# The last two modulation sets of layer two as VectorE sums over feature chunks, in a planned kernel on one core

## Chip, core and metric

One NeuronCore of a Trainium2 chip runs the whole program in one launch. The metric is the device time of one execution in microseconds. Times of instructions, waits and transfers come from one execution that the hardware profiler recorded.

## What is computed

The program is a block of two transformer layers over 256 latent tokens (`x`) and 256 context tokens (`ctx`), followed by a second network of mixers and cross-attention. The part that matters here is the first block, cut down:

```python
silu_c, silu_cc = jax.nn.silu(c), jax.nn.silu(c_ctx)[None]       # 1 x 1024 each
for l in range(2):
    need_ctx = l < 1
    mod   = silu_c  @ w_ada[l] + b_ada[l]                         # 1024 x 6144 weights
    mod_c = silu_cc @ w_ada[l] + b_ada[l]
    sh1, sc1, g1, sh2, sc2, g2 = jnp.split(mod, 6, axis=-1)
    h = modulate(rms_norm(x, norm1_g[l]), sh1, sc1)               # likewise hc from mod_c
    y, yc = mixer_sublayer(h, hc, ..., need_ctx)                  # w_in, attention, branches, w_out
    x = x + g1 * y
    h = modulate(rms_norm(x, norm2_g[l]), sh2, sc2)
    x = x + g2 * expert_choice_ffn(h, ...)                        # 16 experts of 1024 x 1024, three matrices each
    if need_ctx:                                                  # layer one only
        ...                                                       # the same for the context tokens
```

`w_ada[l]` is 24 MB and is used for two vectors alone. Its 6144 columns are six modulation vectors of 1024. The kernel takes them in three sets of two: set 0 is `sh1, sc1`, set 1 is `g1, sh2`, set 2 is `sc2, g2`. In layer two the context tokens need set 0 only, since nothing after their keys and values is computed.

## The kernel before

**The planner.** The kernel writes no order of its own. Every operation goes to a planner (class `Plan`), which builds the graph of dependencies, gives each operation a modelled cost on each engine that may run it, and places all of them by list scheduling on five queues: TensorE, ScalarE, VectorE, GpSimd, and SyncE, which issues the transfers. `copy` may go to ScalarE or VectorE, `binary` to VectorE or GpSimd, `scaled` to ScalarE or VectorE; the planner chooses. The real instructions are all issued from one line of `issue`, line 461, so that the profile shows L461 everywhere and groups are told apart by tile names.

**Weights.** Each weight tile is 1 MB (8 KB per partition) and comes through the ring `W`, which has six buffers (`BUFS`, line 40). `split_stream` loads a tile, calls `step()`, which takes one unit of background work, and splits each 128x512 slice into a rounded half `wh` (a copy, on ScalarE or VectorE) and the rest `wl` (a subtraction, on VectorE or GpSimd). `linear` then makes three products with 512 columns for each slice and each half of the tokens. In the experts the weights go to TensorE unsplit, and the ring is longer: `wring` names the tiles that are free then, 14 in layer one (line 1607) and 17 in layer two (line 1638), six of them `W`.

**Modulation.** `ada_units` gives eight units for a set. Four of them load two tiles of 128x2048 (two `W` buffers) and make 8 products on TensorE: a weight of 128x32, `scT`, which holds both vectors (latent and context), against 512 columns of `w_ada`; the four column groups go to four row groups of one PSUM bank, `acc`. In the trace each such product is two MATMUL records. After the eighth unit, `ada_finish` copies the bank to SBUF on ScalarE, makes four transposes (128x128), four more in `ada_pairs` (the order of features that the router and experts use), and adds biases on VectorE for both streams.

**The stage.** The two sets of layer two that the change touches are background work of layer two's dense stage, 940 to 1217 us of the trace: `dense` makes the queries, keys and values (`w_in`), the attention (about 1020 to 1064 us), the gates and branches, and the product with `w_out`, which needs set 1. Before it stand layer one's dense stages (to 440 us) and its experts (440 to 938 us), after it layer two's experts (1217 to 1650 us) and the second network. The units are hung in at line 1630:

```python
self.bg, self.bgrate = self.ada_units(1, (1, 2)), 1
self.dense(1, 0, xs, hi, lo, self.z_tiles(1536), ctx_prep, lambda: self.mem_norm(0))
```

## Time and profile before

| | |
|---|---|
| runs | 2045.97, 2048.46, 2048.66 us; median 2048.46 |
| the profiled execution | 2050.08 us, its span 2048.3 us |
| TensorE busy (PE) | 1815.9 us, 89% |
| VectorE busy (DVE) | 881.5 us, 43% |
| ScalarE busy (ACT) | 855.3 us, 42% |
| GpSimd busy (POOL) | 300.9 us, 15% |
| moved by DMA | 611.72 MB, mean 299 GB/s |
| granted TensorE clock, mean | 0.937 of full speed |

The stages differ: in the dense stages TensorE is busy nearly all the time, in the experts the transfers run without a break. A share over the whole span hides that; the profile's table by stage, further down, is the one to read. The profiled execution lies 1.62 us above the median of the runs.

### The profile page before, as it was taken

What the parts mean: (1) busy time and instruction counts of PE and PEld (TensorE: products, weight loads), DVE (VectorE), ACT (ScalarE), POOL (GpSimd) and SP (SyncE); (2) the same over time, 40 slices, a digit from 0 to 9 for tenths busy, and PEclk for the clock granted to TensorE, in tenths of its full rate; (3) what the DMA queues carried; (4) which work ended last, traced back from release to release, by engine and by line L of the source; (5) the groups of instructions that cost most, each with busy time, mean ns of one, the idle gap of its engine ahead of it and who ended that gap; (6) DMA issues with size and microseconds to landing.
All of it is one profiled execution on the core that took longest, in us unless ns stands there. A gap on an engine that the chain in (4) does not pass through costs nothing.

```text
span 2048.3 us, 29471 instructions
## 1 busy us (share of the span) xinstructions
PE 1815.9 (89%) x11570; PEld 1148.4 (56%) x11570; DVE 881.5 (43%) x1855; ACT 855.3 (42%) x1895; POOL 300.9 (15%) x387
## 2 busy tenths in 40 slices
PE   7999999999999898878899997666766689999997
PEld 4677767774443232224677774322322268889886
DVE  3766686680020100206765650101000057867775
ACT  3664676562232121114575541101110046776765
POOL 1202250230000000003500300000000023312421
PEclk9999999999999999999999998866667789999999
DMA  9767663678989999998647889999999975436330
GB/s 367 264 224 273 228 237 129 224 274 317 409 368 374 422 402 422 421 421 323 230 183 289 288 338 421 421 421 420 421 421 421 421 275 150 140 119 192 123 124 32
DMA packets 150347, 611.72 MB, mean 299 GB/s; under 512 B 10144, under 2 KB 32320, under 8 KB 96192
## 3 DMA queue, kind: packets, MB, share of 16 engines
q1 hardware_dynamic: 150208, 609.84, 77.5%
q8 instruction: 91, 1.49, 0.3%
q14 instruction: 48, 0.39, 0.1%
HBM read 606.63 MB, written 3.16 MB: 298 GB/s over the span
## 4 chain that ended last, share of the span: by engine, by line
PE 57%; DMA 30%; DVE 7%; POOL 2%; ACT 2%; issue 1%; SPq 0%; POOLq 0%; DVEq 0%; ACTq 0%
PE lin L461 43%; PE aux L461 13%; DMA W<-w_gate_e 5%; DMA W<-w_up_e 4%; DMA W<-w_down_e 3%; PE acc L461 2%; DMA HL<-w_gate_e 2%; DMA OL<-w_up_e 2%; DMA G<-w_down_e 2%; DVE wl L461 2%; DMA M<-w_gate_e 2%; DMA G<-w_gate_e 2%; DMA KC<-w_down_e 1%; POOL sm L461 1%; DVE S L461 1%
## 5 line engine op out<-in xcount | busy, mean ns | idle before, releaser
L461 DVE TENSOR_TENSOR wl<-W,wh 128x512 fp32r<-128x512 f32 (+1 forms) x514 | 360.3, 705 | 162.9 <-ACT wh L461 159.3
L461 ACT ACTIVATE wh<-W 128x512 fp32r<-128x512 f32 (+1 forms) x482 | 291.3, 607 | 241.4 <-PE lin L461 186.5
L461 DVE TENSOR_TENSOR S<-lin,S 128x512 f32<-128x512 f32 (+1 forms) x32 | 17.9, 558 | 596.6 <-PE lin L461 581.5
L461 ACT ACTIVATE S<-lin 32x512 f32<-32x512 f32 (+2 forms) x94 | 52.3, 556 | 421.8 <-PE lin L461 421.0
L461 POOL TENSOR_TENSOR wl<-W,wh 128x512 fp32r<-128x512 f32 (+1 forms) x62 | 80.6, 1302 | 947.7 <-DMA W<-w_in 412.9
L461 PE MATMUL lin<-wl,HH 128*128 128x512 f32 (+1 forms) x600 | 205.6, 394 | 2.8 <-DVE wl L461 2.8
L461 PE MATMUL lin<-wh,HL 128*128 128x512 f32 (+1 forms) x600 | 204.0, 393 | 0.7 <-DVE HL L461 0.7
L461 PE MATMUL lin<-wh,HH 128*128 128x512 f32 (+1 forms) x600 | 203.8, 392 | 0.8 <-ACT wh L461 0.5
L461 PE MATMUL lin<-W,S 128*32 128x256 f32 (+1 forms) x1288 | 149.5, 512 | 49.5 <-DMA W<-w_up_e 14.2
L461 PE MATMUL aux<-cst,S 128*128 128x128 f32 x604 | 116.1, 287 | 23.0 <-DVE S L461 18.4
L461 PEld LDWEIGHTS lin<-W,S 128*32 128x32 f32 (+1 forms) x1288 | 50.7, 133 | 134.3 <-issue 47.3
L461 ACT ACTIVATE S<-aux 128x512 f32<-128x512 f32 (+5 forms) x139 | 66.6, 485 | 141.0 <-PE aux L461 139.7
L461 PEld LDWEIGHTS lin<-wl,HH 128*128 128x128 f32 x600 | 107.9, 189 | 27.9 <-DVE wl L461 8.1
L461 PEld LDWEIGHTS aux<-cst,S 128*128 128x128 f32 x604 | 79.5, 154 | 73.6 <-DVE S L461 42.1
L461 PEld LDWEIGHTS lin<-wh,HH 128*128 128x128 f32 x600 | 108.5, 189 | 20.9 <-issue 3.4
L461 PEld LDWEIGHTS lin<-wh,HL 128*128 128x128 f32 x600 | 108.9, 189 | 18.1 <-DVE HL L461 1.3
L461 PE MATMUL lin<-wh,OL 128*128 128x512 f32 x272 | 93.9, 396 | 0.0
L461 POOL TENSOR_SCALAR sm<-sm 128x1 f32<-128x1 f32 (+3 forms) x42 | 17.1, 407 | 466.3 <-ACT G L461 392.5
L461 ACT ACTIVATE S<-aux,sm 128x256 f32<-128x256 f32 (+2 forms) x136 | 71.4, 529 | 15.4 <-DVE sm L461 12.9
L461 PE MATMUL lin<-wl,OH 128*128 128x512 f32 x208 | 75.5, 402 | 2.4 <-DVE wl L461 2.2
L461 PE MATMUL lin<-wh,OH 128*128 128x512 f32 x208 | 76.2, 403 | 0.0
L461 PE MATMUL lin<-W,HL 128*64 128x512 f32 x288 | 68.4, 601 | 7.4 <-DMA W<-w_up_e 4.7
(430 smaller groups left out, 3264.0 us busy)
## 6 DMA issues: line engine op xcount, KB each, us to landing
W<-w_in SPq DMA_DIRECT2D x62, 1024.0 KB, 7.2
W<-w_up_e SPq DMA_DIRECT2D x50, 1024.0 KB, 18.6
W<-w_gate_e SPq DMA_DIRECT2D x50, 1024.0 KB, 18.7
W<-w_down_e SPq DMA_DIRECT2D x49, 1024.0 KB, 19.7
W<-w_ada SPq DMA_DIRECT2D x40, 1024.0 KB, 5.0
W<-w_in SPq DMA_DIRECT2D x32, 768.0 KB, 4.7
W<-w_out SPq DMA_DIRECT2D x20, 1024.0 KB, 5.1
Z<-w_down_e SPq DMA_DIRECT2D x17, 1024.0 KB, 19.8
```

Of the source, the lines that this page charges most:

```text
L461: fn(*(self.real(a) for a in args), **{k: self.real(a) for k, a in kw.items()})
```

## The change

Sets 1 and 2 of layer two are computed for the latent stream alone, in another way. `ada_sums` gives eight units for a set (two column halves of 1024, four units each). A unit loads one tile with two feature chunks of 128 x 1024 columns (1 MB, one `W` buffer) and VectorE multiplies each by the latent vector's value on its partition and adds it into a tile `ac` (128x1024, two buffers). After four units `ada_block` sums over the partitions on TensorE: for each 128 columns one product with `ac` as the weight and a 128x2 column of ones. Eight products give the half; eight more give the pair order for the half that needs it, so that a set has 24 products and both sets 48. `ada_done` adds the biases straight from PSUM. The copy on ScalarE, the transposes and the context stream's half are gone; `modT[1]` is set to zero once at the start, since the gates' transpose still reads both streams. `ac` takes the 8 KB of one `W` buffer: the ring `W` goes from six to five, everywhere, and the experts' rings from 14 to 13 and from 17 to 16 tiles.

```diff
-BUFS = {"W": (2048, 6), "HH": (2048, 1), "HL": (2048, 1), "OH": (2048, 1), "OL": (2048, 1), "Z0": (2048, 1), "Z1": (2048, 1),
+BUFS = {"W": (2048, 5), "HH": (2048, 1), "HL": (2048, 1), "OH": (2048, 1), "OL": (2048, 1), "Z0": (2048, 1), "Z1": (2048, 1),
...
-        "M": (2304, 1),
+        "M": (2304, 1), "ac": (1024, 2),
...
+        nc.vector.memset(self.modT[1], 0.0)
...
+    def ada_sums(self, r):
...
+        def unit(g, h):
+            if g == 0 and h == 0:
+                box["ps"] = self.acc_ps()
+            if h == 0:
+                box["a"] = self.t([128, 1024], F32, "ac")
+            acc = box["a"]
+            w = self.wload(src, 2 * h, 2, r * 2048 + 1024 * g, 1024)
+            for k in range(2):
+                sc = self.scT[:, 2 * h + k, 0:1]
+                if h or k:
+                    nc.vector.scalar_tensor_tensor(out=acc, in0=w[:, k], scalar=sc, in1=acc, op0=ALU.mult, op1=ALU.add)
+                else:
+                    nc.vector.tensor_scalar(out=acc, in0=w[:, k], scalar1=sc, scalar2=None, op0=ALU.mult)
+            if h == 3:
+                self.ada_block(r, g, acc, box["ps"])
+                if g:
+                    self.ada_done(r, box["ps"])
+        return [lambda g=g, h=h: unit(g, h) for g in range(2) for h in range(4)]
+
+    def ada_block(self, r, g, acc, ps):
...
+        for i in range(8):
+            o = 16 * g + 2 * i
+            self.nc.tensor.matmul(ps[:, o:o + 2], acc[:, 128 * i:128 * i + 128], self.ones2, start=True, stop=True, skip_group_check=True)
+        if g == (r == 1):
+            e = acc.rearrange("p (a q j) -> p a j q", a=4, j=2)
+            for i in range(8):
+                o = 32 + 2 * i
+                self.nc.tensor.matmul(ps[:, o:o + 2], e[:, i // 2, i % 2], self.ones2, start=True, stop=True, skip_group_check=True)
+
+    def ada_done(self, r, ps):
...
+        nc.vector.tensor_tensor(out=self.modT[1][:, cs, 0], in0=v[:, 0:16], in1=self.sml("b_ada", 48, 48)[:, cs], op=ALU.add)
+        o = (self.B2 if r == 1 else self.A2)[1][:, 0, :]
+        nc.vector.tensor_tensor(out=o, in0=v[:, 16:24], in1=self.sml("b2p", 16 + 8 * (r - 1), 8), op=ALU.add)
+        if r == 2:
+            nc.vector.scalar_tensor_tensor(out=o, in0=o, scalar=1.0, in1=self.sml("norm2p", 8, 8), op0=ALU.add, op1=ALU.mult)
+        self.ada_scales(1, r, (0,))
...
-        self.wring = ["DFT", "M", "W", "W", "W", "W", "W", "W", "Z1", "OH", "OL", "Z0", "G0", "G1"]
+        self.wring = ["DFT", "M", "W", "W", "W", "W", "W", "Z1", "OH", "OL", "Z0", "G0", "G1"]
...
-        self.bg, self.bgrate = self.ada_units(1, (1, 2)), 1
+        self.bg, self.bgrate = self.ada_sums(1) + self.ada_sums(2), 1
...
-        self.wring = ["DFT", "M", "KC", "W", "W", "W", "W", "W", "W", "Z1", "OH", "OL", "HL", "HH", "Z0", "G0", "G1"]
+        self.wring = ["DFT", "M", "KC", "W", "W", "W", "W", "W", "Z1", "OH", "OL", "HL", "HH", "Z0", "G0", "G1"]
```

The planner lays the whole program out anew. On TensorE, just ahead of the attention of layer two (the last products of the keys and queries, then the transposes `aux<-cst`; `lin`, `aux` and `acc` are PSUM banks, the number behind a name is its buffer and use), the queue before has six groups of the set's products:

```order
L461 MATMUL lin_1_220<-wh_0_200,HL_5_5599 128x512
L461 MATMUL acc_0_129<-W_3_342,scT 32x512 x4
L461 MATMUL acc_0_129<-W_4_371,scT 32x512 x4
L461 MATMUL aux_3_122<-cst,M_0_485 128x128
L461 MATMUL aux_1_340<-cst,S_2_853 128x128 x2
L461 MATMUL acc_0_129<-W_1_181,scT 32x512 x4
L461 MATMUL acc_0_129<-W_2_323,scT 32x512 x4
L461 MATMUL acc_0_129<-W_5_417,scT 32x512 x4
L461 MATMUL acc_0_129<-W_0_165,scT 32x512 x4
L461 MATMUL aux_2_119<-cst,M_0_485 128x128 x2
L461 MATMUL aux_3_122<-cst,S_0_483 128x128 x4
```

And now, at the same place:

```order
L461 MATMUL lin_1_221<-wh_0_201,HL_5_5600 128x512
L461 MATMUL acc_0_130<-ones_69,ac_0_5524 128x2
L461 MATMUL lin_2_278<-wh_1_203,HH_5_5590 128x512
L461 MATMUL lin_0_218<-wh_1_203,HH_5_5590 128x512
L461 MATMUL acc_0_130<-ones_69,ac_0_5524 128x2 x5
L461 MATMUL aux_1_341<-cst,S_2_870 128x128 x2
L461 MATMUL aux_3_123<-cst,M_0_507 128x128
L461 MATMUL acc_0_130<-ones_69,ac_0_5524 128x2
L461 MATMUL lin_2_278<-wl_1_228,HH_5_5590 128x512
L461 MATMUL aux_2_120<-cst,M_0_507 128x128
```

The groups of four products with 512 columns are gone from here, and products with two columns stand among the linear products, each of them reading an `ac` tile.

On VectorE, in the attention of layer two (the reductions and reciprocals are the softmax's, `OL<-aux` is attention output, `wl` a weight's rest, `S<-S,sm` the softmax's scaling), the queue before reads:

```order
L461 TENSOR_REDUCE sm_9_529<-aux_1_340 128x1
L461 TENSOR_TENSOR wl_1_227<-W_3_342,wh_1_202 128x512
L461 TENSOR_REDUCE sm_12_540<-aux_2_119 128x1
L461 RECIPROCAL sm_11_519<-sm_10_543 128x1
L461 TENSOR_TENSOR OL_19_6059<-aux_3_122,OH_20_6052 128x256
L461 TENSOR_SCALAR S_2_208<-S_2_208,sm_11_519 128x512
L461 TENSOR_REDUCE sm_18_818<-aux_1_340 128x1
L461 TENSOR_REDUCE sm_15_807<-aux_3_122 128x1
L461 TENSOR_TENSOR OL_19_6059<-aux_0_177,OH_20_6052 128x256
L461 RECIPROCAL sm_14_798<-sm_13_780 128x1
L461 TENSOR_TENSOR wl_2_215<-W_4_371,wh_2_205 128x512
```

And now, some rows into the same softmax:

```order
L461 SCALAR_TENSOR_TENSOR ac_1_5852<-W_3_343,scT,ac_1_5852 128x1024
L461 TENSOR_REDUCE sm_15_804<-aux_3_123 128x1
L461 TENSOR_REDUCE sm_18_826<-aux_1_341 128x1
L461 RECIPROCAL sm_14_798<-sm_13_788 128x1
L461 SCALAR_TENSOR_TENSOR ac_1_5852<-W_0_166,scT,ac_1_5852 128x1024
L461 RECIPROCAL sm_17_820<-sm_16_815 128x1
L461 RECIPROCAL sm_20_848<-sm_19_837 128x1
L461 TENSOR_REDUCE sm_21_857<-aux_3_123 128x1
L461 TENSOR_REDUCE sm_0_100<-aux_1_341 128x1
L461 SCALAR_TENSOR_TENSOR ac_1_5852<-W_0_166,scT,ac_1_5852 128x1024
L461 COPY S_2_870<-aux_0_178 128x4x128
L461 SCALAR_TENSOR_TENSOR ac_1_5852<-W_2_324,scT,ac_1_5852 128x1024
```

Sums into `ac` stand between the reductions, where subtractions for weights and scalings stood; most of these went to GpSimd and ScalarE.

On the transfers' queue, where layer two's dense stage ends and the experts' weights begin (`W_n` are the ring's buffers, the other names tiles that are free by then), before:

```order
L461 DMA W_3_342<-w_down_e 128x2048
L461 DMA W_4_371<-w_down_e 128x2048
L461 DMA kv<-QB_5_7492 128x1024
L461 DMA W_5_417<-w_down_e 128x2048
L461 DMA QB_6_7569<-w_gate_e 128x1024
L461 DMA W_0_165<-w_down_e 128x2048
L461 DMA M_0_485<-w_down_e 128x2048
L461 DMA G_24_7630<-w_up_e 128x2048
L461 DMA G_20_7659<-w_up_e 128x2048
L461 DMA DFT_17_7686<-w_down_e 128x2048
L461 DMA KC_5_7712<-w_down_e 128x2048
L461 DMA W_1_181<-w_down_e 128x2048
```

And now:

```order
L461 DMA W_4_372<-w_up_e 128x2048
L461 DMA W_0_166<-w_down_e 128x2048
L461 DMA kv<-QB_5_7491 128x1024
L461 DMA W_1_182<-w_down_e 128x2048
L461 DMA QB_6_7557<-w_gate_e 128x1024
L461 DMA W_2_324<-w_down_e 128x2048
L461 DMA M_0_507<-w_down_e 128x2048
L461 DMA G_25_7627<-w_up_e 128x2048
L461 DMA G_21_7656<-w_up_e 128x2048
L461 DMA DFT_18_7683<-w_up_e 128x2048
L461 DMA KC_5_7709<-w_down_e 128x2048
L461 DMA W_0_166<-w_gate_e 128x2048
```

Before, the names go round the six buffers, W_5 among them; now the ring comes back to W_0 after W_4, and by the end of the excerpt a buffer (W_0) is given out for the second time, which the excerpt of before does not do.

## Rows read from the trace of the kernel before

**Rows 1.** Busy time by stage; the first line names the columns.

```profile
core 0: us, PE busy (x) PEld busy (x) DVE busy (x) ACT busy (x) POOL busy (x), PEclk, DMA share, GB/s
635.00:938.00 303.00, 260.96 (x1136) 86.16 (x1134) 29.32 (x46) 48.37 (x88) 0.00 (x0) 0.98 1.00 415
946.00:1020.00 74.00, 66.16 (x331) 47.09 (x330) 59.56 (x109) 46.95 (x95) 44.44 (x71) 0.98 0.71 258
1020.00:1064.00 44.00, 44.00 (x309) 35.99 (x309) 34.35 (x85) 36.12 (x86) 3.36 (x3) 1.00 0.40 144
1064.00:1217.00 153.00, 151.46 (x892) 116.94 (x895) 93.48 (x184) 83.98 (x162) 25.17 (x25) 1.00 0.81 297
1217.00:1650.00 433.00, 303.03 (x3170) 129.59 (x3164) 26.40 (x47) 49.53 (x128) 2.56 (x4) 0.74 1.01 420
1650.00:2048.30 398.30, 377.45 (x2456) 330.92 (x2448) 291.69 (x633) 268.81 (x653) 107.63 (x141) 0.98 0.43 137
```

**Rows 2.** Instructions writing acc in 900 to 1250 us: min/median/max ns, first and last start.

```profile
L461 PE MATMUL acc<-W,scT x128: 592/592/617, 973.2 to 1142.4; 128*32 128x512 f32 x128
```

**Rows 3.** TensorE in order of time: start, duration, idle before and its releaser.

```profile
1005.80 3.64 PE L461 MATMUL acc<-W,scT 128*32 128x512 f32 x32
1012.18 0.44 PE L461 MATMUL aux<-cst,M 128*128 128x128 f32 x2 [2.74 <-DVE KC L461]
1014.96 1.25 PE L461 MATMUL aux<-DFT,S 128*128 128x128 f32 x4 [1.78 <-DVE QB L461]
```

**Rows 4.** The same view in the experts of layer one, and in the attention of layer two.

```profile
526.57 1.05 PE L461 MATMUL aux<-ones,S 128*128 128x2 f32 x8
527.55 1.08 PE L461 MATMUL lin<-G,HH 128*64 128x512 f32 x4
...
554.67 0.38 PE L461 MATMUL aux<-ones,S 128*128 128x2 f32 x2
554.98 1.94 PE L461 MATMUL lin<-W,S 128*64 128x512 f32 x8
...
1025.69 0.60 PE L461 MATMUL aux<-cst,S 128*128 128x128 f32 x4
1026.05 0.48 PE L461 MATMUL aux<-KC,QA 128*128 128x256 f32 x2
```

**Rows 5.** VectorE and GpSimd groups by shape, whole span: busy us, mean ns, idle before.

```profile
L461 DVE SCALAR_TENSOR_TENSOR S<-x,sm,KC 128x1024 f32<-128x1024 f32 x2 | 2.6, 1284 | 1.3 <-POOL sm L461 1.3
...
L461 DVE TENSOR_SCALAR Z<-XC,sm 128x1024 f32<-128x1024 f32 x2 | 1.5, 754 | 5.4 <-POOL sm L461 5.4
...
L461 DVE TENSOR_SCALAR Z<-x,sm 128x1024 f32<-128x1024 f32 x3 | 4.2, 1406 | 1.2 <-POOL sm L461 1.2
...
L461 DVE TENSOR_TENSOR wl<-W,wh 128x512 fp32r<-128x512 f32 x396 | 292.8, 743 | 135.2 <-ACT wh L461 131.8 <-DMA W<-w_br_global 0.5 <-issue 0.2
...
L461 DVE CAST wh<-W 128x512 fp32r<-128x512 f32 x76 | 37.8, 499 | 7.6 <-PE lin L461 6.6 <-PE aux L461 0.2
...
L461 DVE TENSOR_SCALAR S<-S,sm 128x512 f32<-128x512 f32 x27 | 13.3, 496 | 0.7
...
L461 POOL TENSOR_TENSOR wl<-W,wh 128x512 fp32r<-128x512 f32 x52 | 70.0, 1350 | 522.7 <-ACT wh L461 347.2 <-DVE wh L461 175.4
```

**Rows 6.** Busy time in two stretches of ten us in the experts of layer one.

```profile
580.00:590.00 10.00, 10.00 (x47) 3.32 (x45) 5.84 (x9) 4.95 (x9) 0.00 (x0) 1.00 0.61 253
...
620.00:630.00 10.00, 10.00 (x48) 3.38 (x46) 0.00 (x0) 2.96 (x7) 0.00 (x0) 1.00 0.53 197
```

**Rows 7.** The DMA queue's own waits, 540 to 640 us: total us, times, longest.

```profile
SPq L461 <- PE lin L461: 68.5, 8, 13.6
```

**Rows 8.** Busy time at the start of the experts of layer two.

```profile
1200.00:1210.00 10.00, 10.00 (x63) 7.62 (x63) 3.39 (x7) 3.64 (x7) 0.00 (x0) 1.00 0.72 265
...
1220.00:1230.00 10.00, 10.00 (x186) 5.93 (x178) 0.85 (x2) 1.94 (x6) 0.00 (x0) 1.00 0.99 412
```

**Rows 9.** The DMA queue's own waits, 1150 to 1217 us.

```profile
SPq L461 <- DVE wl L461: 17.2, 5, 7.1
```

**Rows 10.** VectorE's waits for a weight load, 940 to 1215 us.

```profile
DVE wl L461 <- DMA W<-w_br_global: 0.5, 1, 0.5
```

More of the change, by code (lines that the diff above doesn't have):

```diff
@@ L873, in ada_units @@
         return units
+    def ada_sums(self, r):
+        nc = self.nc
+        src = self.A["w_ada"][1]
+        box = {}
+        def unit(g, h):
[26 more added lines that the diff above has]
+    def ada_done(self, r, ps):
+        nc = self.nc
+        cs = slice(r * 16, r * 16 + 16)
+        v = ps[:, 0:48].rearrange("p (i w) -> p i w", w=2)[:, :, 0]
+        nc.vector.tensor_tensor(out=self.modT[1][:, cs, 0], in0=v[:, 0:16], in1=self.sml("b_ada", 48, 48)[:, cs], op=ALU.add)
[4 more added lines that the diff above has]
+        self.ada_scales(1, r, (0,))
     def ada_first(self):
@@ L927, in ada_finish, with ada_scales @@
             nc.vector.tensor_tensor(out=o, in0=i0, in1=b, op=ALU.add)
-        for s in range(2):
+        self.ada_scales(l, r, (0, 1))
+    def ada_scales(self, l, r, streams):
+        nc = self.nc
+        mod = self.modT[l]
+        for s in streams:
             if r == 0:
```

## The prediction

> **What bounds the kernel now.** I read the table by stage first, since the shares of the whole span mix stages with different limits [rows 1]. Two stages run at the transfers' rate: the end of layer one's experts (635 to 938 us, DMA share 1.00 at 415 GB/s) and layer two's experts (1217 to 1650 us, 1.01 at 420 GB/s); TensorE is busy 261 of 303 and 303 of 433 us there, so what ends them is the bytes still to come. Layer two's dense stage, where the change sits, goes by TensorE once attention has begun: 44.00 of 44 us from 1020, 151.46 of 153 from 1064. Ahead of the attention, 946 to 1020, it is mixed: TensorE 66.16 of 74, VectorE 59.56, and the last waits there, 2.74 us for VectorE's KC and 1.78 us for its QB, stand right behind two groups of modulation products [rows 3]. In that stretch VectorE's chain, not TensorE's work, sets when attention starts. Then I looked at where the six W buffers matter: as lead for weights in the dense stages, and as part of the ring that holds expert weights when an expert stage begins.
>
> **TensorE.** The old sets are 128 records [rows 2], 8 groups of 16; two groups last 3.64 us [rows 3], so a group is 1.82 us and all are 14.6 us. Their 16 transposes go by the row of other 128x128 products, four records starting 0.36 us before the next work, 0.09 us each [rows 4]: 1.4 us. Added are 48 products of two columns. The row of such products (`ones`) has eight records, two for each product, that take 0.98 us up to the next start [rows 4], 0.245 us a product; two records alone take 0.31 us. 48 x 0.245 = 11.8 us, at most 14.9. Net -14.6 - 1.4 + 11.8 = **-4.2 us** (-1.1 at the dear price). Where it lies matters: the first old group starts at 973.2 us and the first four stand ahead of attention, where by the new order only 8 of the 48 products stand. Ahead of attention that is -7.3 + 2.0 = -5.3 us on an engine that already waits for VectorE; behind it -7.3 - 1.4 + 9.8 = +1.1 us on an engine that is full.
>
> **VectorE.** 32 operations of 128x1024 are new: 28 multiply-and-add, 4 multiply. The trace has two multiply-and-adds of that shape at 1284 ns; a multiply of that shape takes 754 ns in one group and 1406 ns in another [rows 5]. I take 1284 and 754, since the operands (SBUF, a scalar for each partition) are those of these rows: 36.0 + 3.0 = 39.0 us, 41.6 with 1406. In exchange the planner moves 18 subtractions `wl` to GpSimd (743 ns each on VectorE, 1350 ns there [rows 5]) and takes over 9 casts `wh` from ScalarE at 499 ns. Dense stage in sum: 39.0 - 13.4 + 4.5 = **+30 us** on VectorE, and 18 x 1.35 = +24 us on GpSimd. By the order it falls so. Ahead of attention: 9 x 1.284 + 2 x 0.754 - 3 x 0.743 + 2 x 0.499 = +11.9 us, on 59.56 of 74: 71.5 of 74. In attention: 12 x 1.284 + 0.754 - 9 x 0.743 - 11 scalings x 0.496 (to ScalarE) + 6 x 0.499 = +7.0 us, on 34.35 of 44: 41.4 of 44. Later: +5.7 on 93.48 of 153, which has room. Each time it just fits. But VectorE's queue is in order: a sum that waits for its 1 MB tile, or runs, holds the softmax's reductions and reciprocals behind it, and TensorE waits for those. So the 5.3 us that TensorE gets back ahead of attention I cost at nothing: they end at VectorE, whose 14.4 us of idle time become 2.5. Bounds: -5 if the cover holds, +9 if one sum of 1.284 us in three of the 21 up to the end of attention delays TensorE by its own length.
>
> Here GpSimd and VectorE would work side by side more than before. In 946 to 1020 us they were busy 59.56 + 44.44 = 104 us in 74, so at least 30 us overlapped [rows 1]; the trace shows no general exclusion between them. The Trainium skill's page "SBUF — State Buffer" states under "Who interferes with whom" that the port pair these two engines share is an exclusive lock, and that a VectorE instruction with two SBUF inputs contends with a GpSimd instruction that reads SBUF. The added multiply-and-adds are such instructions, and so are the subtractions moved to GpSimd, so the rule speaks against the change; the 30 us say that it can't hold for everything both run. What it would cost is rival D.
>
> **The transfers.** The bytes of the two sets are the same, 16 tiles of 1 MB. Layer two's dense stage uses two W buffers for a pair of tiles before and one a unit after, with five in the ring. Its weights are early now: between 940 and 1215 us VectorE waited for a weight tile once, 0.5 us [rows 10]. With five buffers I take +1 us for this and all other dense stages and the second network (-2 to +4; five sixths of a lead that hardly ever runs out).
>
> The experts are another matter. Before their unbroken stretch the transfers stop because the ring is full: 253 GB/s in 580 to 590 us and 197 in 620 to 630 [rows 6], the transfers' queue waiting 68.5 us in eight waits for TensorE's `lin` products to release tiles [rows 7]. From 635 us on nothing stops them until the stage's end. A tile less in the ring is 1.049 MB less held when that stretch begins, and at 0.42 MB/us (420 GB/s) that is **2.5 us** later at the end. In layer two the queue waits 17.2 us for VectorE's `wl` (W tiles still in use by the dense stage) before 1217 us [rows 9], the rate is 265 GB/s in 1200 to 1210 and 412 from 1220 on [rows 8]: again a tile less, **2.5 us**. Bounds 0 (another tile comes free in time, or a full ring wasn't what held the last tile back) to 5 each.
>
> **The sum.** Dense stage of layer two: 0 ahead of and in attention, +1.1 behind it; experts +2.5 and +2.5; other stages +1: +7.1 us on the profiled execution's 2050.08 = 2057.2. That execution lies 1.62 us above the median, so the forecast for the median is **2055.5 us**, 0.3% slower.
>
> **Rivals.** (B) The VectorE work does fit into its idle time, so TensorE's -4.2 counts, and the experts' +5 balance it: about 2049.3, no change. For it: VectorE stays at 71.5 of 74 and 41.4 of 44 and the order was laid out for just that. Against it: the planner's modelled costs, and waits right ahead of attention that are VectorE's now. (C) The other side: TensorE's gain is larger than its net, because some 12 of the 48 small products fall into idle time it has anyway (7.8 us ahead of attention), -4.2 - 12 x 0.245 = -7.1, and the experts lose nothing since the tile that is missing wasn't the last to come free: about 2041.4, faster. It decides if the experts' unbroken stretches begin as early, measured from the stage's start, as before. (D) GpSimd and VectorE stop each other: while a sum runs, a GpSimd subtraction doesn't. Up to the end of attention 21 sums of 1.284 us are 27 us; GpSimd was busy 44.44 + 3.36 = 47.8 of those 118 us, 0.40, so 0.40 x 27 = 10.9 us of waiting more, and TensorE waits for these `wl`. On the forecast: about 2066.4. It decides if the mean of GpSimd's `wl` rises well over 1350 ns or the sums over 1284. By the skill's rule named above this is the expected case; the 30 us of overlap are against its full size.
>
> **How the numbers follow.** A 0.42, B 0.24, C 0.20, D 0.14. The range reaches from C's inner edge to D: C lies at 2041.4 with an upper half that reaches 2044 (less than 12 products in idle time), so 2043 to 2065 leaves out about half of C and half of D, 0.17. Under 0.2%, 4.1 us, a measurement of this kernel can't tell a difference from none. Faster by more (under 2044.4): most of C and a little of B, 0.20. Within (up to 2052.6): B and the lower part of A, 0.32. Slower: the rest of A, and D, 0.48.
>
> **What would show it.** Right: `acc<-W,scT` gone from 940 to 1217 us; `ac` operations at about 1.28 us; VectorE near 71 of 74 ahead of attention and near 41 of 44 in it; the dense stage as long as before within 3 us; both expert stages' unbroken stretches ending some 2.5 us later after their dense stage's end. Wrong: a dense stage shorter by 4 us or more with VectorE's idle time left (B, C); the products of two columns at well over 0.31 us, or TensorE idle behind `ac`; TensorE waiting for GpSimd's `wl` or for reciprocals in attention (D); expert stages of the same length (C); waits for W tiles in layer one or the second network, where I put 1 us.

## The result and the profile after

The changed kernel takes 2070.16 us (median; 2066.89 to 2071.72) against 2048.56 us for the kernel before: ratio 1.0101, interval 1.0083 to 1.0119. That is 1.0% or about 21 us slower. The forecast was 7 us slower, with 2065 as the upper end. The profiled execution of the changed kernel took 2066.89 us, 3.3 us under its median, with a span of 2065.1; the traces therefore show 16.8 of the 21 us.

Where they arise is read from the last residual addition of each stage (`x<-x,S` at the end of a dense stage, `x<-aux,x` at the end of the experts). In order of time on VectorE, before (start, duration):

```profile
438.81 0.68 DVE L461 TENSOR_TENSOR x<-x,S 128x512 f32<-128x512 f32 x1
...
950.18 0.68 DVE L461 TENSOR_TENSOR x<-aux,x 128x512 f32<-128x512 f32 x1
...
1182.22 0.67 DVE L461 TENSOR_TENSOR x<-x,S 128x512 f32<-128x512 f32 x1
...
1661.88 0.69 DVE L461 TENSOR_TENSOR x<-aux,x 128x512 f32<-128x512 f32 x1 [0.28 <-PE aux L461]
```

And after:

```profile
445.54 0.67 DVE L461 TENSOR_TENSOR x<-x,S 128x512 f32<-128x512 f32 x1
...
959.89 0.68 DVE L461 TENSOR_TENSOR x<-aux,x 128x512 f32<-128x512 f32 x1
...
1197.23 0.68 DVE L461 TENSOR_TENSOR x<-x,S 128x512 f32<-128x512 f32 x1
...
1681.08 0.69 DVE L461 TENSOR_TENSOR x<-aux,x 128x512 f32<-128x512 f32 x1 [0.28 <-PE aux L461]
```

Each stage's length is the distance between the ends (start plus duration):

| stage, us | before | after | difference | forecast |
|---|---|---|---|---|
| layer one's dense stages (from the start) | 439.5 | 446.2 | +6.7 | part of one "+1" |
| layer one's experts | 511.4 | 514.4 | +3.0 | +2.5 |
| layer two's dense stage | 232.0 | 237.3 | +5.3 | +1.1, and part of the "+1" |
| layer two's experts | 479.7 | 483.9 | +4.2 | +2.5 |
| the rest, to the end of the span | 385.7 | 383.3 | -2.4 | part of the "+1" |

A stage read from one execution is uncertain by some 2 us; the control below shows this.

In layer two's dense stage the busy times of the whole stage are, before and after (columns as in [rows 1]):

```profile
950.86:1182.90 232.04, 224.02 (x1232) 171.05 (x1231) 163.01 (x322) 147.64 (x302) 67.91 (x90) 0.99 0.70 252
```

```profile
960.56:1197.91 237.35, 225.18 (x1172) 178.23 (x1171) 198.29 (x319) 149.92 (x304) 106.80 (x107) 0.96 0.70 246
```

TensorE's idle time there rises from 8.0 to 12.2 us, and its granted clock falls from 0.99 to 0.96, which over 225 busy us is some 7 us more. Since its busy time rises by only 1.2 us, its work at equal clock is some 5 or 6 us less (an estimate from these rows): the saving that the forecast put at 4.2 us is there, and is spent again on clock and waits. VectorE is up by 35 us, where +30 were forecast, and GpSimd by 39, where +24 were.

The changed kernel reaches this place some ten us late, so the stretches have to be counted from the stage's start and from the attention's first score product on TensorE:

```profile
1019.86 0.48 PE L461 MATMUL aux<-KC,QA 128*128 128x256 f32 x2
```

```profile
1030.32 0.78 PE L461 MATMUL aux<-KC,QA 128*128 128x256 f32 x2
```

Ahead of it, 44 us from it on, and the rest of the stage; before and after:

```profile
950.86:1019.86 69.00, 62.47 (x315) 45.19 (x315) 54.68 (x103) 43.64 (x90) 40.50 (x65) 0.98 0.69 248
1019.86:1063.86 44.00, 44.00 (x311) 35.99 (x310) 34.49 (x85) 36.12 (x86) 3.50 (x3) 1.00 0.40 144
1063.86:1182.90 119.04, 117.55 (x611) 89.88 (x609) 73.85 (x135) 67.88 (x128) 23.91 (x23) 1.00 0.81 293
```

```profile
960.56:1030.32 69.76, 60.30 (x258) 45.50 (x256) 62.39 (x98) 43.05 (x87) 55.22 (x69) 0.91 0.60 212
1030.32:1074.32 44.00, 43.82 (x266) 34.76 (x265) 41.61 (x69) 34.81 (x76) 13.24 (x7) 0.95 0.71 246
1074.32:1197.91 123.59, 121.07 (x654) 97.97 (x653) 94.29 (x154) 72.06 (x142) 38.35 (x31) 0.99 0.75 264
```

The stretch ahead of attention is nearly as long as before, but TensorE is idle for 9.5 us of it instead of 6.5, at a clock of 0.91 instead of 0.98, so that less of its work is done when attention begins. VectorE's added busy time is 7.7 us ahead of attention, 7.1 in its first 44 us and 20.4 behind it; the forecast had 11.9, 7.0 and 5.7. The chain just ahead of attention shows TensorE's waits (in order of time):

```profile
1017.99 1.17 PE L461 MATMUL acc<-ones,ac 128*128 128x2 f32 x10
1020.71 0.66 PE L461 MATMUL aux<-cst,S 128*128 128x128 f32 x2 [1.54 <-POOL S L461]
...
1027.07 1.23 PE L461 MATMUL aux<-DFT,S 128*128 128x128 f32 x4 [0.61 <-DVE QB L461]
1029.55 1.12 PE L461 MATMUL aux<-cst,S 128*128 128x128 f32 x4 [1.26 <-DVE S L461]
```

In [rows 3] there were gaps of 2.74 and 1.78 us at this place. Now shorter ones follow one another, behind GpSimd's and VectorE's S and VectorE's QB. The ten us ahead of the first score product and the ten us from it on, before and after:

```profile
1009.86:1019.86 10.00, 5.90 (x26) 4.91 (x27) 8.74 (x17) 6.46 (x15) 4.59 (x8) 0.83 0.74 273
1019.86:1029.86 10.00, 10.00 (x75) 9.29 (x74) 9.16 (x23) 8.38 (x21) 0.93 (x1) 1.00 0.69 248
```

```profile
1020.32:1030.32 10.00, 7.29 (x24) 5.23 (x24) 9.70 (x22) 5.79 (x14) 8.41 (x12) 0.52 0.21 80
1030.32:1040.32 10.00, 10.00 (x53) 8.66 (x52) 8.85 (x13) 7.16 (x16) 1.27 (x1) 0.79 0.29 105
```

0.52 is for the most part the lower of the clock's two levels (1.2 and 2.4 GHz). By these rows the low clock takes 0.48 x 7.29 + 0.21 x 10 = 5.6 us here and 0.17 x 5.90 = 1.0 us before (an estimate), so it is most of the stage's 5.3 us. The idle time alone doesn't set it: before, TensorE was idle for longer in its ten us, 4.1 against 2.7. Why the clock falls further and stays low for longer here is not settled by these rows.

The operations themselves, VectorE's and then GpSimd's groups over the whole span (busy us, mean ns; compare [rows 5]):

```profile
L461 DVE TENSOR_TENSOR wl<-W,wh 128x512 fp32r<-128x512 f32 x376 | 281.7, 754 | 113.0 <-ACT wh L461 110.6
L461 DVE SCALAR_TENSOR_TENSOR ac<-W,scT,ac 128x1024 f32<-128x1024 f32 x28 | 45.8, 1636 | 0.6 <-DMA W<-w_ada 0.5
...
L461 DVE TENSOR_SCALAR ac<-W,scT 128x1024 f32<-128x1024 f32 x4 | 3.5, 872 | 0.3 <-PE acc L461 0.3
...
L461 POOL TENSOR_TENSOR wl<-W,wh 128x512 fp32r<-128x512 f32 x72 | 105.2, 1467 | 468.2 <-ACT wh L461 336.9 <-DVE wh L461 122.5 <-DVE sm L461 8.6
```

A sum takes 1636 ns in the mean and not 1284, the moved subtraction 1467 instead of 1350. The products of two columns have nearly the forecast's price; their group on TensorE in the dense stage, two records each:

```profile
L461 PE MATMUL acc<-ones,ac 128*128 128x2 f32 x96 | 13.2, 227 | 0.0
```

13.2 us, where 11.8 were forecast and 14.9 at most.

### The profile page after: what moved, and what is told of

Its sections match the earlier page's. It is cut to its first block, busy times and chain, and to the rows that moved or that the text cites. A ratio compares the mean times of both kernels' runs of the same rounds, so it can differ in the third digit from the quotient of the medians.

```text
span 2065.1 us, 29418 instructions
## 1 busy us (share of the span) xinstructions
PE 1820.1 (88%) x11522; PEld 1156.1 (56%) x11522; DVE 924.3 (45%) x1865; ACT 855.0 (41%) x1890; POOL 345.6 (17%) x406
## 5 line engine op out<-in xcount | busy, mean ns | idle before, releaser
L461 DVE TENSOR_TENSOR wl<-W,wh 128x512 fp32r<-128x512 f32 (+1 forms) x491 | 347.5, 712 | 139.2 <-ACT wh L461 136.5
L461 ACT ACTIVATE wh<-W 128x512 fp32r<-128x512 f32 (+1 forms) x469 | 283.7, 607 | 236.3 <-PE lin L461 182.4
L461 POOL TENSOR_TENSOR wl<-W,wh 128x512 fp32r<-128x512 f32 (+1 forms) x85 | 119.8, 1414 | 904.4 <-ACT wh L461 772.5
L461 PE MATMUL lin<-W,S 128*32 128x256 f32 (+1 forms) x1176 | 134.9, 504 | 46.5 <-DMA W<-w_up_e 16.2
L461 PE MATMUL aux<-cst,S 128*128 128x128 f32 (+1 forms) x588 | 118.2, 290 | 23.6 <-DVE S L461 19.6
L461 ACT ACTIVATE S<-aux 128x512 f32<-128x512 f32 (+4 forms) x136 | 64.6, 483 | 175.5 <-PE aux L461 175.1
L461 PEld LDWEIGHTS aux<-cst,S 128*128 128x128 f32 (+1 forms) x588 | 79.1, 155 | 74.3 <-DVE S L461 41.5
L461 PEld LDWEIGHTS lin<-W,S 128*32 128x32 f32 (+1 forms) x1176 | 45.3, 131 | 123.7 <-issue 39.1
L461 DVE TENSOR_REDUCE sm<-aux 128x1 f32<-128x256 f32 (+3 forms) x136 | 65.6, 499 | 24.2 <-PE aux L461 23.4
```

Source lines behind the costliest of these rows:

```text
L461: fn(*(self.real(a) for a in args), **{k: self.real(a) for k, a in kw.items()})
```

## The experiments

Two theories were to be told apart: R, that the weight buffer taken from the ring costs most, and M, that the sums on VectorE do. A third, P, was that the planner's order changes for any reason and the time by chance. Differences below are ratios of each kernel to the kernel before on the same chip, times 2048 us. Stage lengths come from the same residual additions as above.

**Five buffers alone.** The rings and nothing else (the experts' rings lose one W each, too):

```diff
-BUFS = {"W": (2048, 6), ...
+BUFS = {"W": (2048, 5), ...
...
```

> The kernel before with five W buffers and the experts' rings of 13 and 16 tiles; the modulation sets are computed as before. Theory R (the buffer taken from the ring costs most of the 21 us: in the two traces layer one's second dense stage ends 6.7 us later, layer one's experts add about 3 and layer two's experts about 4): 10 to 16 us slower than before. Theory M (the sums on VectorE cost most, and the ring only what was forecast, 6 us): 0 to 6 us slower. Theory P (the planner lays out the whole program anew and chance decides): anything between -5 and +10 in no relation to the other kernels.

Measured: 1.0100 (1.0085 to 1.0115), 20 us slower, as much as the whole change, and above what any of the theories expected. Layer one's dense stages end at 446.1 us, as in the changed kernel (446.2); layer two's dense stage lasts 240.5 us, longer than in the changed kernel (237.3).

**The sums alone, with six buffers.** The sums in the two halves of XC, the rings as before:

```diff
+        self.ac = self.t([128, 2, D], F32, "XC")
...
-                box["a"] = self.t([128, 1024], F32, "ac")
+                box["a"] = self.ac[:, g]
```

> The changed kernel with six W buffers and the experts' rings of 14 and 17 tiles again; the two sums take the halves of the context tokens' tile XC, which is free by then. Theory R: 3 to 7 us slower than before (the dense stage of layer two alone). Theory M: 12 to 18 us slower. By the forecast's net on TensorE alone (VectorE's work hidden): 4 us faster.

Measured: 1.0038 (1.0023 to 1.0053), 7.8 us slower. Layer one is as before (439.3 us), and all of the loss is in layer two's dense stage, 240.6 us against 232.0:

```profile
948.55:1189.18 240.63, 223.32 (x1174) 176.85 (x1174) 198.80 (x314) 151.27 (x308) 113.41 (x111) 0.97 0.68 242
```

TensorE is idle for 17.3 us there instead of 8.0. The loss lies ahead of attention: that stretch lasts 80.9 us instead of 69.0, with VectorE busy for 74.58 us of it and GpSimd for 69.76:

```profile
948.55:1029.45 80.90, 65.89 (x299) 49.99 (x299) 74.58 (x99) 47.50 (x95) 69.76 (x79) 0.94 0.61 224
```

So the sums alone cost 8 us, the buffer alone 20, and both together 21: the costs don't add. Neither R nor M had said so, though 7.8 is near R's upper end of 7.

**Five buffers in layer two's dense stage only.** The sums' tile serves as a sixth weight buffer elsewhere:

```diff
+        self.wring = ["W"] * 5 + ["ac"]
...
+        self.wring, self.wseq = ["W"], 0
+        self.bg, self.bgrate = self.ada_sums(1) + self.ada_sums(2), 1
```

> The changed kernel, but the sums' tile serves as a sixth weight buffer wherever no sums are made: all dense stages except layer two's, both experts' rings (14 and 17), the second network. Only layer two's dense stage has five. Theory R: 5 to 9 us slower than before. Theory M: 13 to 18 us. The distance to the run with six buffers everywhere is what the sixth buffer is worth in layer two's dense stage: 1 to 3 us by the forecast.

Measured: 1.0033 (1.0023 to 1.0044), 6.8 us slower, the stage 239.7 us. With sums, five or six buffers in that stage make no difference; the sixth matters elsewhere.

**A small addition as control.**

```diff
+        nc.vector.memset(self.modT[1], 0.0)
```

> The kernel before with one small addition: the memset of layer two's modulation tile at the start, as the change has it. Theories R and M: the time of before within 2 us. Theory P: the planner's order moves in many places for so small a cause and the time differs by 3 to 7 us in either direction.

Measured: 0.9999 (0.9989 to 1.0008). This is no test of P: but for the memset, the trace holds the same instructions in the same order as before on TensorE, VectorE, ScalarE and GpSimd. It shows instead how far two executions of one order differ: layer one's dense stages end at 441.7 us (before: 439.5), layer two's lasts 233.4 (232.0), and the clock in the ten us ahead of attention is 0.66 (0.83).

**Do five buffers cost so much because of the pairs?** The old sets load two tiles and use them together. With five buffers, one at a time, in layer two only:

```diff
-                for kk in (k - 1, k):
+                ks = (k,) if l and r else (k - 1, k)
+                for kk in ks:
```

> Five W buffers with the products of before, but layer two's sets 1 and 2 take one weight tile at a time instead of two together. Theory Q (with five buffers the old sets cost more because a pair holds two of five buffers at once, so that the sums, one buffer at a time, win back there what they cost): layer two's dense stage some 3 us shorter than with five buffers and pairs, 16 to 19 us slower than before in all. Rival (the number of buffers counts, not how the sets take them): 20 to 22 us slower, as five buffers with pairs.

Measured: 1.0054 (1.0037 to 1.0071), 11 us slower instead of 20, more gained than Q expected. Layer two's dense stage goes from 240.5 to 233.5 us. One of the transfer queue's own waits, that for the sets' products (`acc`) from 950 to 1040 us, goes with it. Total us, times, longest; before, with five buffers in pairs, and with five buffers singly:

```profile
SPq L461 <- PE acc L461: 7.2, 4, 5.2
```

```profile
SPq L461 <- PE acc L461: 19.7, 4, 14.2
```

```profile
SPq L461 <- PE acc L461: 3.9, 4, 2.2
```

With pairs the queue stands 19.7 us, once 14.2 us (1016.6 to 1030.8), until TensorE has used a pair and frees its two buffers. TensorE waits 6.7 us at once for VectorE ahead of attention (1017.0 to 1023.7), where before it was 2.7 [rows 3]:

```profile
PE aux L461 <- DVE KC L461: 6.7, 1, 6.7
```

The queue's long wait ends after TensorE's, so it didn't cause it. What differs is the work that could have filled TensorE's wait: between 50 and 71 us after the stage's start the queue issued four tiles of `w_in` before, one with pairs and five buffers, and five with single tiles. That the pairs bring this about is argued, not shown; the queue's other waits in the same stretch, for VectorE's `wl`, are longer where the stage is shorter (70.3, 45.1 and 65.9 us).

In the changed kernel the queue waits for the sums (`ac`) instead, 16.8 us in four waits, at most 5.9 at once. That the sums so take the place of what the pairs cost may be why the two don't add in layer two; no run separates it.

The same in both layers:

```diff
-                if k % 2 == 0:
-                    return
-                for kk in (k - 1, k):
+                ks = (k,)
+                for kk in ks:
...
```

> Five W buffers, products as before, every modulation set of both layers taking one weight tile at a time. Theory Q (with five buffers it is the pairs of tiles that cost): layer one's dense stages, 6.6 us late with five buffers, end within 2 us of before, the whole 3 to 6 us slower than before. Rival N (in layer one the number of buffers itself counts): 9 to 13 us slower, as with single tiles in layer two alone.

Measured: 1.0038 (1.0025 to 1.0050), 7.8 us slower. Layer one's dense stages end at 441.1 us, 1.6 late instead of 6.6, as Q expected, though the whole came out at 8 rather than 3 to 6, since layer two's dense stage (235.2) and both experts' stages are longer than before. And in the changed kernel itself, where only layer one and set 0 of layer two still use products, the same edit:

> The changed kernel with one edit: the sets that are still made by products (layer one's, and set 0 of layer two) take one weight tile at a time. Theory Q: 5 to 7 us faster than the changed kernel, 14 to 16 us slower than before. Rival N: as the changed kernel, 21 us slower.

Measured: 1.0077 (1.0062 to 1.0092), 16 us slower instead of 21, with layer one at 441.5 us.

**Is a single tile better with six buffers too?** The same edit in the kernel before:

> The kernel before (six buffers) with every set taking one weight tile at a time. If a pair costs with six buffers too: 2 to 5 us faster than before. If a pair costs only where the ring is short: within 2 us.

Measured: 1.0036 (1.0023 to 1.0050), 7.4 us slower: neither expectation. Layer one ends at 445.7 us, as late as with five buffers and pairs, and layer two's dense stage lasts 237.6. So no rule like "single tiles are better" or "more buffers are better" holds: with single tiles five buffers are even a little better in layer one. A tile's lead (from its landing to its first use) doesn't explain it either: worked out roughly over the weight tiles of layer one's dense stages, it is some 4 to 5 us shorter than before in the mean with five buffers, in pairs as with single tiles, and 1 to 2 us shorter with six and single tiles, so that kernels that are 6 us late have either lead.

What layer one's end does go with is the planner's order. Up to 420 us the 17 traces hold six different orders of the instructions on TensorE, VectorE and ScalarE (the memset aside), and kernels with the same order end together:

| rings and tiles of the order | kernels | layer one's dense stages end, us |
|---|---|---|
| six buffers, pairs | before; control; a seventh buffer; set 2 by sums; all sums with the ban on GpSimd | 439.5, 441.7, 439.7, 439.8, 439.9 |
| six buffers, pairs | all sums; before with the ban; the last kernel below | 439.3, 439.0, 438.2 |
| five W and `ac`, pairs | the sums' tile as sixth buffer | 438.7 |
| five buffers, pairs | the changed kernel; rings alone; single tiles in layer two only; changed with the ban | 446.2, 446.1, 445.8, 445.7 |
| five buffers, single | rings alone; the changed kernel | 441.1, 441.5 |
| six buffers, single | before; set 2 by sums with the ban | 445.7, 446.0 |

The 6 us are therefore real. Three orders with six buffers and pairs end alike, which speaks against mere chance; but for each of the other rows there is one order alone, so whether the ring, the way of taking tiles or the order that the planner happened to find makes the 6 us isn't shown. Theory P is not refuted for layer one.

Some of the 6 us can be placed, in layer one's second attention. Before and after:

```profile
270.00:280.00 10.00, 7.90 (x52) 3.29 (x50) 8.87 (x21) 6.48 (x13) 9.06 (x14) 1.00 1.00 374
280.00:290.00 10.00, 8.54 (x57) 7.45 (x58) 9.09 (x16) 8.12 (x20) 5.53 (x7) 1.00 0.62 210
```

```profile
270.00:280.00 10.00, 6.05 (x27) 2.85 (x23) 8.98 (x20) 5.04 (x10) 9.32 (x17) 0.66 0.67 270
280.00:290.00 10.00, 9.55 (x55) 5.54 (x47) 9.31 (x18) 5.85 (x15) 6.77 (x8) 0.82 0.58 210
```

TensorE is busy 7.90 us of the first ten before and 6.05 after, where it waits 3.0 us for VectorE's M, and the clock there is 1.00 and 0.66. In the changed kernel the low clock is worth 0.34 x 6.05 + 0.18 x 9.55 = 3.8 us in these rows (an estimate), and TensorE's idle time up to the stage's end is 1.6 us more than before (14.7 against 13.0 from 40 us on): 5.4 of the 6.7. With six buffers and single tiles (7.47 us at 0.83) the same two are 1.3 and 1.5 us, of 6.2, so that more than half isn't assigned. The few busy us alone don't make a kernel late: with all sums and six buffers TensorE is busy 7.45 us of the same ten, at a clock of 1.00, and layer one ends at 439.3. Why the planner's order comes out so for these rings is not settled by the runs.

**A seventh buffer** in layer two's dense stage:

```diff
+        self.wring, self.wseq = ["W"] * 6 + ["XC"], 0
         self.bg, self.bgrate = self.ada_units(1, (1, 2)), 1
```

> The kernel before, with a seventh weight buffer in layer two's dense stage alone (the tile XC of the context tokens, free there). If buffers count there as the step from six to five says (about 8 us in that stage), and the step from seven to six has half of it: 2 to 6 us faster than before. If six are enough: within 2 us.

Measured: 1.0003 (0.9993 to 1.0013). Six are enough in that stage.

**Where the sums stand.** Six buffers, set 1 by products, set 2 by sums:

```diff
-        self.bg, self.bgrate = self.ada_sums(1) + self.ada_sums(2), 1
+        self.bg, self.bgrate = self.ada_units(1, (1,)) + self.ada_sums(2), 1
```

> Six W buffers; set 1 by products on TensorE as before, set 2 alone by sums on VectorE (16 of the 32), which stand from the attention on. Theory V (the sums cost because VectorE has no room ahead of attention, where it sets when attention starts): 0 to 2 us slower than before, or up to 2 faster, since ahead of attention all is as before. Theory H (every sum costs alike, wherever it stands): half of what six buffers with all sums cost, 4 us slower.

Measured: 0.9994 (0.9985 to 1.0004), no change, against 7.8 us with all sums. V holds: these 16 sums start between 1032 and 1082 us, and cost nothing to be seen, though seven of their 14 multiply-and-adds took 1.65 to 2.32 us instead of 1.28. With all sums and six buffers, set 1's 16 stand between 953 and 1009 us, ahead of attention; they, or the two sets together, carry the 8 us.

**VectorE and GpSimd.** The trace of the changed kernel shows VectorE's sums near 1115 us in order of time,

```profile
1114.07 1.27 DVE L461 SCALAR_TENSOR_TENSOR ac<-W,scT,ac 128x1024 f32<-128x1024 f32 x1
1115.26 0.68 DVE L461 SCALAR_TENSOR_TENSOR Z<-G,lin 128x512 f32<-128x512 f32 x1
1115.86 1.72 DVE L461 SCALAR_TENSOR_TENSOR ac<-W,scT,ac 128x1024 f32<-128x1024 f32 x1
1117.50 0.68 DVE L461 COPY S<-aux 128x512 f32<-128x512 f32 x1
1118.10 0.67 DVE L461 SCALAR_TENSOR_TENSOR Z<-G,lin 128x512 f32<-128x512 f32 x1
1118.69 2.38 DVE L461 SCALAR_TENSOR_TENSOR ac<-W,scT,ac 128x1024 f32<-128x1024 f32 x1
1121.00 0.15 DVE L461 TENSOR_TENSOR B<-acc,small 128x8 f32<-128x8 f32 x1
1121.07 1.17 DVE L461 COPY B<-modT 128x8 f32<-128x8 f32 x1
1122.16 2.37 DVE L461 SCALAR_TENSOR_TENSOR ac<-W,scT,ac 128x1024 f32<-128x1024 f32 x1
```

and GpSimd in the same stretch:

```profile
1114.95 8.50 POOL L461 TENSOR_TENSOR wl<-W,wh 128x512 fp32r<-128x512 f32 x5 [30.09 <-ACT wh L461]
```

The sum at 1114.07, begun before GpSimd's subtractions, takes 1.27 us. Those that start among them take 1.72, 2.38 and 2.37, and GpSimd's five subtractions 8.50 us, 1.70 each, where [rows 5] has 1.35. Sums that ran with nothing on GpSimd all took 1.26 to 1.29 us. Over the whole changed kernel, 11 sums that began during one of GpSimd's subtractions took 1.72 to 2.38 us, 10.0 us more in all; and of the 72 subtractions, the 13 that began during a sum took 1.96 us in the mean, the others 1.36. Whoever comes second waits. The Trainium skill says so on the page "SBUF — State Buffer", section "Who interferes with whom": the port pair is an exclusive lock, and a VectorE instruction with two SBUF inputs contends with a GpSimd instruction that reads SBUF. The trace agrees with it, 2.38 against 1.27 us. The kernel before had it already, between two subtractions: one of VectorE's takes 0.69 us with nothing on GpSimd, and the 19 that began during one of GpSimd's took 1.21 in the mean, up to 1.77. To price it, the weights' rests were kept off GpSimd in this stage, with six buffers:

```diff
-        self.binary(wl, w, wh.bitcast(F32), ALU.subtract)
+        if self.vonly:
+            self.nc.vector.tensor_tensor(out=wl, in0=w, in1=wh.bitcast(F32), op=ALU.subtract)
+        else:
+            self.binary(wl, w, wh.bitcast(F32), ALU.subtract)
```

> All sums with six W buffers, and in layer two's dense stage the weights' rests (wl) on VectorE alone, none on GpSimd. Theory L (VectorE and GpSimd hold each other up: a sum that starts while a GpSimd subtraction runs takes 2.2 to 2.4 us instead of 1.28): every sum at 1.26 to 1.35 us. On the time: if the holding up is worth more than the 15 to 20 us of subtractions that come back to VectorE, faster than with GpSimd's help (0 to 6 us slower than before); otherwise 10 to 16 us slower than before.

Measured: 1.0019 (1.0010 to 1.0028), 3.9 us slower instead of 7.8; the stage 232.7 us instead of 240.6, though VectorE took the subtractions back (4 are left on GpSimd in the stage, of 29). "Every sum at 1.26 to 1.35" did not come true, since other GpSimd instructions remain (1350 ns in the mean, against 1457 with the subtractions there). The same ban in the changed kernel:

> The changed kernel (five buffers, all sums) with the weights' rests on VectorE alone in layer two's dense stage. If GpSimd's subtractions and the sums hold each other up there as they do with six buffers (7.5 us slower than before with GpSimd, 3.9 without): 3 to 8 us faster than the changed kernel, 13 to 18 us slower than before. If with five buffers the stage is short of tiles and not of VectorE: as the changed kernel, within 2 us.

Measured: 1.0060 (1.0046 to 1.0074), 12.3 us slower instead of 20.7: the ban is worth 8 us, a little more than expected. The sums' group in the dense stage,

```profile
L461 DVE SCALAR_TENSOR_TENSOR ac<-W,scT,ac 128x1024 f32<-128x1024 f32 x28 | 36.7, 1311 | 1.1 <-DMA W<-w_ada 1.1
```

has 1311 ns a sum instead of 1636. And in the kernel before, as the control:

> The kernel before (products, six buffers) with the same ban on GpSimd in that stage. If the gain of the ban comes from the sums being held up: no gain here, 0 to 3 us slower, since 7 to 25 subtractions come back to VectorE for nothing. If GpSimd's subtractions are a bad bargain in any case: 1 to 4 us faster.

Measured: 0.9990 (0.9981 to 0.9999), 2 us faster, without any sum. So the ban gives 8 us with the sums and five buffers, 4 with the sums and six, and 2 without sums; but it moves 26, 25 and 11 subtractions, so how much of the 8 and the 4 comes from sums and subtractions holding each other up isn't separated. A rival is the subtraction itself, which takes 1.29 us on GpSimd (median) and 0.69 on VectorE alone, and which TensorE waits for. With the sums and six buffers, TensorE's waits in the stage have these two rows, of which the kernel before has the second alone, with 1.9 us:

```profile
PE lin L461 <- POOL wl L461: 5.3, 4, 2.0
PE lin L461 <- DVE wl L461: 4.3, 8, 1.2
```

In the changed kernel the first is 3.1 us, and with the ban 2.6 us (six buffers) and 1.5 us (five).

**A version that avoids both.** Set 2 by sums, set 1 by products, six buffers, the ban, and every product set with single tiles:

```diff
-        self.bg, self.bgrate = self.ada_sums(1) + self.ada_sums(2), 1
+        self.bg, self.bgrate = self.ada_units(1, (1,)) + self.ada_sums(2), 1
+        self.vonly = True
...
+                ks = (k,)
+                for kk in ks:
```

> The three findings together: six buffers, sets by products take single tiles, set 2 of layer two alone by sums on VectorE, and in that dense stage the weights' rests on VectorE alone. Theory: 3 us (GpSimd no longer holds the sums up) and 1 to 2 us (single tiles) less than with set 2 by sums alone: 3 to 6 us faster than before. If the parts don't add: within 2 us of before.

Measured: 0.9991 (0.9982 to 1.0001), so in the whole the parts don't add. Layer two's dense stage is 227.2 us, 4.9 shorter than before, but layer one, also with single tiles, ends at 446.0. With pairs in layer one again:

```diff
-                ks = (k,)
+                ks = (k,) if l and r else (k - 1, k)
```

> Six buffers; set 2 of layer two by sums, set 1 by products with single tiles, the ban on GpSimd in that stage; layer one with pairs as before, so that its dense stages end as before (439 us in the profile, not 446). If the stages add: 227 us for layer two's dense stage as with single tiles everywhere, 5 to 7 us faster than before. If layer one's later end was hidden in the experts anyway: 2 us faster, as before this edit.

Measured: 0.9962 (0.9948 to 0.9976), 2040.38 us, 8 us faster than before, and the fastest of all. Layer one's dense stages end at 438.2 us and layer two's lasts 225.7:

```profile
947.24:1172.89 225.65, 218.79 (x1200) 170.48 (x1199) 179.24 (x335) 152.08 (x307) 56.12 (x76) 1.00 0.72 257
```

TensorE has 6.9 us of idle time and the full clock. Its 14 multiply-and-adds in this stage:

```profile
L461 DVE SCALAR_TENSOR_TENSOR XC<-W,scT,XC 128x1024 f32<-128x1024 f32 x14 | 17.8, 1274 | 0.0
```

1274 ns each, none held up. No run has the same kernel with set 2 by products, so what the sums, the single tiles and the ban each give in it isn't separated.

## Why the forecast was wrong

**The direction held, the size didn't**: slower, but by three times the forecast and 5 us beyond the range.

**TensorE's term held**: 13.2 us for the new products, 11.8 forecast, and the old groups are gone. What it saved went into TensorE's waits and clock.

**The first failed step is the price of the buffer in the dense stages**, "+1 us for this and all other dense stages and the second network", with +4 as its bound. The changed kernel loses 6.7 us in layer one alone, where only the rings differ; with the rings alone it is +6.6 there and +8.5 in layer two's dense stage. The step reasoned from one missing wait [rows 10]: tiles are early, so a sixth less lead is harmless. The waits for weight tiles are in fact still missing. The time went where such a wait can't show it: the planner writes another order around five buffers ahead of time, in which TensorE waits for VectorE instead and its clock falls. Taking single tiles gives back 9 of the 20 us in layer two and 13 in both layers, so with five buffers most of the loss goes with the pairs; but with six buffers single tiles cost 7 us, so this is no rule, and why each order comes out as it does stays open.

**The second is the cover on VectorE.** The +11.9 us ahead of attention and the +7.0 in it were costed at nothing because they "just fit". The busy times came out near these (+7.7 and +7.1; the sum of +30 left out the 11 scalings, with which the three parts make 24.6), and still the sums alone cost 8 us with six buffers, near the dear end of the bounds (-5 to +9) that the text itself gave: the stretch ahead of attention lasted 80.9 us instead of 69.0, since what TensorE waits for there stands in VectorE's and GpSimd's queues, and a sum can delay it though the engine has idle time left. Part of it is the sum's duration, 1284 ns forecast from a row during which no GpSimd subtraction ran, 1636 measured: 28 x 0.35 = 10 us more on VectorE. The forecast had this as rival D, with 10.9 us up to the end of attention and a chance of 0.14. Its signs came: sums over 1284, `wl` on GpSimd over 1350, TensorE waiting for it. Its size is not measured cleanly: among the first 21 sums, which it counted, 5.5 of the 10 us fall, and the ban gives 8, 4 or 2 us. Its mechanism was half of what the trace shows: the subtraction waits for the sum, and as much the sum for the subtraction, and so VectorE's whole queue behind it. That "30 us overlapped" was read as a reason against it was the error: busy time of two engines overlaps also while one of them is held up. The durations of VectorE's own subtractions, 0.69 and 1.21 us, would have shown it in the trace of before.

**The experts' terms were of the right size**, +3.0 and +4.2 where +2.5 each were forecast. One trace is uncertain by as much as the difference, but all together say the same: the six with 13 and 16 tiles have 513.1 and 482.2 us in the mean, the eleven with 14 and 17 have 510.3 and 479.1, which is +2.7 and +3.1.

**Rivals B and C fell**: VectorE's work did not hide, and what TensorE saved did not shorten the stage. In the forecast the terms added up; in the runs 20 and 8 make 21, perhaps since the sums take away the pairs that five buffers make dear. The forecast had the direction from the experts' terms, which held; most of the loss came from the two terms that it had at next to nothing. About 4 us between the profiled executions and the medians are put down to no stage.

## What to carry to other kernels

A buffer that is "never waited for" is not spare when a scheduler orders the work around it: price it by a run with that one number changed, and by more than one order, since one edit can bring an order that is 6 us worse. Ask how many buffers one step holds at once. Before moving work to an engine with idle time, look at what its neighbour runs in the same stretch, and put the work where the engine's queue isn't what TensorE waits for.

## What the runs showed of the hardware

A VectorE multiply-and-add of 128x1024 with two inputs in SBUF takes 1.26 to 1.29 us alone and up to 2.38 us if it starts during a GpSimd subtraction of 128x512, whose own time rises from 1.29 us (median) to 1.96 in the mean if it starts during a sum, and to 2.33 at most in the changed kernel. Two subtractions of 128x512 do it too: VectorE's takes 0.69 us alone, up to 1.77 if it starts during GpSimd's (kernel before). A copy of 128x8 took 1.17 us in the same crowd, and 0.15 to 0.29 us elsewhere. In the ten us ahead of attention TensorE was idle for 4.1 us at a clock of 0.83 before, 2.7 at 0.66 in a second execution of the same order, and 2.7 at 0.52 in the changed kernel, where the next ten us had 0.79: the idle time alone does not tell the clock.
